# Stick-breaking attention inside a mixer block: another form for the score products, one pass for the value products, the scan in place

## The chip, the cores and the metric

The kernel runs on one core of one Trainium2 chip. A run's time is the device time of one execution in microseconds (us). The three runs of the kernel before are 2158.82, 2163.37 and 2165.51 us; their median, 2163.37 us, is the time that the change is measured against.

## The reference

A model block of width 1024 works on 512 positions. Its input projection feeds two groups of eight heads of 64 columns each: a recurrent group (RWKV-7 time mixing) and a stick-breaking attention group. Both outputs go through one output projection; a second model follows, of a conv layer and a neighbourhood-attention layer, each with an FFN. The change touches the stick-breaking group:

```python
q, k, v, g = jnp.split(p, 4, axis=-1)                  # 8 heads of 64 columns
z = jnp.einsum('bhqd,bhkd->bhqk', q_blk, k) / 8        # one block of 128 queries
mask = k_pos[None, :] < q_pos[:, None]                 # strictly causal
log_1m = jnp.where(mask, jax.nn.log_sigmoid(-z), 0.0)
after = lax.cumsum(log_1m, axis=3, reverse=True) - log_1m
attn = jnp.where(mask, jnp.exp(jax.nn.log_sigmoid(z) + after), 0.0)
o = jnp.einsum('bhqk,bhkd->bhqd', attn, v)             # then RMS norm per head, times silu(g)
```

The modulation vectors that several layers use (`mod = silu(c) @ w_ada + b_ada`) are the other place that the change touches.

## The kernel before, in words

Everything is float32. Large products are made of three f32r products of high and low parts (`mm3`, L171 to L173): a weight is loaded by DMA to `st`, ScalarE (ACT) casts it to a high part `wh` (L155), VectorE (DVE) subtracts to get the low part `wl` (L156), and TensorE (PE) adds hi*hi, lo*hi and hi*lo in one PSUM bank. Small products are plain f32; the profile shows each of those as two instructions on PE.

`block1` makes four recurrent pairs of heads (`rwkv_pair`, 0 to 3) and four attention pairs (`sb_pair`, 4 to 7) in the order of the table `ORDER`; then, from L435, the output projection. A scheduling layer sorts each engine's instructions ahead of time: what is written earlier has priority, and where that waits, the next ready work is put between. So the products of a later recurrent pair, or of the output projection, stand on PE between the steps of an attention pair. Each engine then runs its list in order.

An attention pair `p` goes like this. Two projections give q and k as plain f32 tiles (L1046). Every second pair makes the values `sbv`. A third projection gives the gate, on which ACT takes a sigmoid (L1069, L1070). Then come four query blocks i with two heads e each, eight rounds of one chain over the first n = 128(i+1) keys:

- PE: the score product (L1078), f32, in which the head's 64 rows of q and k are contracted, so on 64 of the array's 128 rows; then a bf16 product that adds the causal mask (L1079)
- ACT: two sigmoids out of PSUM (L1082, L1083)
- DVE: a memset of one column (L1085), a reversed running product into the tile `cum` (L1087), a product (L1089)
- PE: i+1 transposes (L1093); DVE for e = 0 or ACT for e = 1 copies them out of PSUM to `pt` (L1095)

The scores and the transposes share one PSUM bank (`ss`). After each query block its value products follow (L1100): 128 queries wide, f32, on 64 of the array's columns, one for each j up to i and each head. The pair ends in a norm (L1103 to L1111).

The modulation sums (`ada_load`, `ada_sum`, L193 to L209) are DVE work that is spread over `block1` at low priority and over the conv layer and the first FFN (`step`, two jobs at a time): GpSimd (POOL) issues a DMA of one 128x1024 row block to the tile `ast` (two buffers), and DVE reduces it in two halves, for each of one or two condition vectors.

Of the kernel before, what the change touches and what calls it, by code (L numbers as in the profile page):

```python
# [15 lines left out]
D = 1024  # L16
KT = 8
S = 512
# [66 lines left out]
class K:  # L85
# [98 lines left out]
    def cact(self, i):  # L184
# [3 lines left out]
        t = self.ap.tile([128, D], F32, tag="ast", name="ct", bufs=2)  # L188
        nc.scalar.activation(t, c, AF.Tanh, scale=0.5)
        nc.vector.scalar_tensor_tensor(c, t, 1.0, c, op0=ALU.add, op1=ALU.mult)  # L190
        return c

    def ada_load(self, src, cbs, mod, bname, j):  # L193
        st = self.ap.tile([128, D], F32, tag="ast", name="ast", bufs=2)
        self.nc.gpsimd.dma_start(st, src)  # L195
        return st, cbs, mod, bname, j

    def ada_sum(self, job, after=None):
        st, cbs, mod, bname, j = job
        for hf in range(2):  # L200
            hs = slice(512 * hf, 512 * hf + 512)
            for r, c in enumerate(cbs):
# [3 lines left out]
                    out=junk, in0=st[:, hs], in1=c[:, hs], scale=0.5, scalar=o if hf else self.V(bname, j),  # L206
# [105 lines left out]
    def block1(self):  # L312
# [524 lines left out]
    def rwkv_pair(self, p, W, h, zl, omu, oka, pre):  # L837
# [45 lines left out]
        XY = T("XY", (128, NCH, 2, CH), 2)  # L883
# [152 lines left out]
    def sb_pair(self, p, W, h, sbt):  # L1036
# [4 lines left out]
        qk = []  # L1041
        for i in range(2):
            t = sb.tile([128, S], F32, tag=f"qk{i}", name=f"qk{i}")
            ps = self.psum("acc")
            self.gemm(ps, W[17 + 4 * i + p], h)
            nc.scalar.mul(t, ps, 0.125 if i == 0 else 1.0)  # L1046
            qk.append(t)
        q, k = qk
# [17 lines left out]
        pg = self.psum("acc")  # L1066
        self.gemm(pg, W[25 + p], h)
        gs = sb.tile([128, S], F32, tag="sgs", name="sgs")
        nc.scalar.activation(gs, pg, AF.Sigmoid)  # L1069
        TT(gs, gs, pg, ALU.mult)  # L1070
        po = self.psum("so")
        for i in range(4):
            n = 128 * (i + 1)
            pts = []
            for e in range(2):
                r = slice(64 * e, 64 * e + 64)
                pz = self.psum("ss")
                mm(pz[:, :n], lhsT=q[r, 128 * i:n], rhs=k[r, :n], start=True, stop=False)  # L1078
# [11 lines left out]
                pT = self.psum("ss")  # L1090
# [115 lines left out]
```

## Time and profile before

The profile is of one execution: its span, from first to last instruction, is 2157.0 us. No device time of this execution stands beside it; the median of the runs is 6.4 us above the span.

| what | value |
|---|---|
| runs, median | 2163.37 us |
| profiled execution, span | 2157.0 us |
| PE busy | 2099.8 us, 97% of the span |
| DVE busy | 1237.6 us, 57% |
| ACT busy | 805.3 us, 37% |
| granted TensorE clock, mean | 0.990 |
| first score product, last score product | at 122 us and 489 us |

PE is the engine that nearly always works; a PE matmul's duration includes its way through the array, so the distance from one start to the next tells what it costs in a row of matmuls. DVE is busy for a little over half of the whole, but for much more in the attention stretch.

### The profile page before, as it was taken

What the parts mean: (1) busy time and instruction counts of PE and PEld (TensorE: products, weight loads), DVE (VectorE), ACT (ScalarE), POOL (GpSimd) and SP (SyncE); (2) the same over time, 40 slices, a digit from 0 to 9 for tenths busy, and PEclk for the clock granted to TensorE, in tenths of its full rate; (3) what the DMA queues carried; (4) which work ended last, traced back from release to release, by engine and by line L of the source; (5) the groups of instructions that cost most, each with busy time, mean ns of one, the idle gap of its engine ahead of it and who ended that gap; (6) DMA issues with size and microseconds to landing.
All of it is one profiled execution on the core that took longest, in us unless ns stands there. A gap on an engine that the chain in (4) does not pass through costs nothing.

```text
span 2157.0 us, 34034 instructions
## 1 busy us (share of the span) xinstructions
PE 2099.8 (97%) x13824; PEld 1673.6 (78%) x13824; DVE 1237.6 (57%) x2598; ACT 805.3 (37%) x1503; POOL 173.8 (8%) x241
## 2 busy tenths in 40 slices
PE   6999999998999999999999999899999999999999
PEld 3676667665788887888888888797777777888887
DVE  2869886657987738643453454525554545434443
ACT  3436444346322225221221222416565635323232
POOL 0000000003200001000000000101222211000000
PEclk9999999999999999999999999999999999999999
DMA  7432322113344412331332232121110112232323
GB/s 269 145 100 89 109 71 79 34 46 99 109 153 149 147 50 98 123 122 65 122 115 88 101 120 83 63 69 59 40 58 32 45 59 79 98 98 95 100 97 99
DMA packets 61934, 203.62 MB, mean 94 GB/s; under 512 B 6993, under 2 KB 9041, under 8 KB 61777
## 3 DMA queue, kind: packets, MB, share of 16 engines
q1 hardware_dynamic: 46800, 146.92, 20.1%
q0 software_dynamic: 14976, 54.53, 7.4%
q8 instruction: 108, 1.77, 0.3%
q14 instruction: 50, 0.40, 0.1%
HBM read 199.32 MB, written 2.10 MB: 93 GB/s over the span
## 4 chain that ended last, share of the span: by engine, by line
PE 89%; DVE 5%; ACT 3%; DMA 1%; issue 1%; SPq 0%; POOL 0%; ACTq 0%; DVEq 0%; POOLq 0%
PE acc L172 19%; PE acc L173 19%; PE acc L171 19%; PE cacc L173 5%; PE cacc L172 5%; PE cacc L171 5%; PE py L826 2%; DVE nt L285 2%; PE sm L804 2%; PE pT L817 2%; PE sm L802 1%; PE ss L1078 1%; PE so L1100 1%; PE G L910 1%; PE py L1014 1%
## 5 line engine op out<-in xcount | busy, mean ns | idle before, releaser
L155 ACT CAST wh<-st 128x512 fp32r<-128x512 f32 (+2 forms) x481 | 292.2, 609 | 721.8 <-PE acc L172 283.2
L156 DVE TENSOR_TENSOR wl<-st,wh 128x512 fp32r<-128x512 f32 (+2 forms) x481 | 324.0, 676 | 352.5 <-ACT wh L155 350.1
L171 PE MATMUL acc<-xzzh,wh 128*128 128x512 f32 x352 | 138.7, 394 | 0.0
L173 PE MATMUL acc<-xzzh,wl 128*128 128x512 f32 x352 | 138.0, 392 | 0.0
L172 PE MATMUL acc<-xzzl,wh 128*128 128x512 f32 x352 | 138.0, 392 | 0.0
L205 DVE CUSTOM_DVE_ANT_0 junk<-ast,cb,vec 128x512 bf16<-128x512 f32 x168 | 125.2, 745 | 3.3 <-DMA ast<-in_w_ada_dram 1.9
L205 DVE CUSTOM_DVE_ANT_0 junk<-ast,cb,m 128x512 bf16<-128x512 f32 x168 | 125.4, 747 | 2.3
L195 POOL DMA_DIRECT2D ast<-in_w_ada_dram x96 | 50.8, 529 | 865.4 <-DVE m L205 781.0
L173 PEld LDWEIGHTS acc<-xzzh,wl 128*128 128x128 f32 x352 | 66.0, 188 | 14.8
L171 PEld LDWEIGHTS acc<-xzzh,wh 128*128 128x128 f32 x352 | 66.1, 188 | 13.5 <-issue 0.5
L172 PEld LDWEIGHTS acc<-xzzl,wh 128*128 128x128 f32 x352 | 66.1, 188 | 13.5 <-issue 0.5
L171 PE MATMUL acc<-h0h,wh 128*128 128x512 f32 (+1 forms) x164 | 66.1, 406 | 4.2 <-ACT h0h L292 2.9
L172 PE MATMUL cacc<-czzl,wh 128*128 128x256 f32 x240 | 68.0, 284 | 0.0
L172 PE MATMUL acc<-h2l,wh 128*128 128x512 f32 (+1 forms) x164 | 66.2, 404 | 1.7 <-DVE h2l L293 1.7
L171 PE MATMUL cacc<-czzh,wh 128*128 128x256 f32 x240 | 67.5, 281 | 0.0
L172 PE MATMUL acc<-h1l,wh 128*128 128x512 f32 (+1 forms) x164 | 66.9, 408 | 0.6 <-POOL h1l L290 0.5
L173 PE MATMUL cacc<-czzh,wl 128*128 128x256 f32 x240 | 67.4, 281 | 0.0
L172 PE MATMUL acc<-h0l,wh 128*128 128x512 f32 (+1 forms) x164 | 66.2, 404 | 0.3 <-DVE h0l L293 0.3
L171 PE MATMUL acc<-h4h,wh 128*128 128x512 f32 (+1 forms) x164 | 65.3, 398 | 1.2 <-ACT h4h L292 0.8
L173 PE MATMUL acc<-h2h,wl 128*128 128x512 f32 (+1 forms) x164 | 66.2, 404 | 0.0
L172 PE MATMUL acc<-h6l,wh 128*128 128x512 f32 (+1 forms) x164 | 65.4, 399 | 0.7 <-DVE h6l L293 0.7
L173 PE MATMUL acc<-h0h,wl 128*128 128x512 f32 (+1 forms) x164 | 66.1, 403 | 0.0
(783 smaller groups left out, 5672.8 us busy)
## 6 DMA issues: line engine op xcount, KB each, us to landing
ast<-in_w_ada_dram POOLq DMA_DIRECT2D x96, 512.0 KB, 4.0
st<-in_ffn_w_in_dram SPq DMA_DIRECT2D x88, 512.0 KB, 3.5
st<-in_ffn_w_out_dram SPq DMA_DIRECT2D x32, 448.0 KB, 3.3
st<-in_w_in_dram SPq DMA_DIRECT2D x24, 512.0 KB, 3.5
st<-in_conv_w_in_dram SPq DMA_DIRECT2D x24, 512.0 KB, 4.4
ast<-in_ada_n_dram SPq DMA_DIRECT2D x16, 512.0 KB, 9.0
st<-in_ffn_w_out_dram SPq DMA_DIRECT2D x16, 512.0 KB, 3.5
st<-in_w_qk_dram SPq DMA_DIRECT2D x16, 512.0 KB, 3.5
```

The lines of the kernel that those rows point to most:

```text
L155: nc.scalar.copy(hi[:, :n], sl)
L156: nc.vector.tensor_tensor(lo[:, :n], sl, hi[:, :n].bitcast(F32), ALU.subtract)
L171: mm(out, lhsT=lh, rhs=rh, start=first, stop=False)
L172: mm(out, lhsT=lh, rhs=rl, start=False, stop=False)
L173: mm(out, lhsT=ll, rhs=rh, start=False, stop=last)
L195: self.nc.gpsimd.dma_start(st, src)
L205: i = self.nc.vector.tensor_tensor_reduce(out=junk, in0=st[:, hs], in1=c[:, hs], scale=0.5, scalar=o if hf else self.V(bname, j), op0=ALU. ...
L285: nc.vector.scalar_tensor_tensor(t, xs[k], gain[:, k:k + 1], rstd, op0=ALU.mult, op1=ALU.mult)
L802: mm(o[e], lhsT=qh[:, e, qs], rhs=ks(kk[:, e]), start=True, stop=False)
L804: mm(o[e], lhsT=ql[hv[e], qs], rhs=ks(kk[hv[e], e]), start=False, stop=True)
L817: nc.tensor.transpose(pT[:, i], s[:, 128 * i:128 * i + 128], self.C("ident"))
L826: mm(g(po[64 * e:64 * e + 64]), lhsT=vb, rhs=pr.rearrange("p (a t) -> p a t", a=2) if j == 0 else pr, start=n == 0, stop=n == 3)
```

## The change

Scores. q and k are kept as high and low f32r parts. The keys of a pair lie in tiles of two slots, one for each head; the other head's 64 rows of a slot are zero (written once by POOL). Each score product becomes three f32r products that contract all 128 rows. The two parts of q take one ACT and one DVE instruction, those of k two and two on 64 rows each.

Scan. The running product is written over its input, `om`, and the product that follows takes it shifted by one column; the tile `cum` and its memset are gone.

Values. The transposed weights of all four query blocks are kept, ordered by key block, and the value products come after the eighth round: one for each key block and head, 512, 384, 256 and 128 queries wide. The copies out of PSUM are made in two pieces where i > 1.

Gate. Its projection and sigmoid stand behind the value products.

Space. `XY` of the recurrent pairs has one buffer in place of two. A modulation row comes as two half rows in two 512-column tiles; `ast` has still two buffers, which now hold one row together. The tanh of the condition vectors goes by halves.

```diff
     def ada_load(self, src, cbs, mod, bname, j):
-        st = self.ap.tile([128, D], F32, tag="ast", name="ast", bufs=2)
-        self.nc.gpsimd.dma_start(st, src)
+        st = []
+        for hs in (slice(0, 512), slice(512, D)):
+            t = self.ap.tile([128, 512], F32, tag="ast", name="ast", bufs=2)
+            self.nc.gpsimd.dma_start(t, src[:, hs])
+            st.append(t)
...
+            self.kz = [[sb.tile([128, 2, S], F32R, name=f"kz{n}") for n in "hl"]]
+            for t in self.kz[0]:
+                nc.gpsimd.memset(t[64:128, 0].bitcast(F32), 0.0)
+                nc.gpsimd.memset(t[0:64, 1].bitcast(F32), 0.0)
...
-        XY = T("XY", (128, NCH, 2, CH), 2)
+        XY = T("XY", (128, NCH, 2, CH))
...
-            nc.scalar.mul(t, ps, 0.125 if i == 0 else 1.0)
+        nc.scalar.mul(qh, ps, 0.125)
+        STT(ql, ps, 0.125, qh.bitcast(F32), op0=ALU.mult, op1=ALU.subtract)
...
+        for e, r in enumerate(hv):
+            nc.scalar.copy(kh[r, e], ps[r])
+            TT(kl[r, e], ps[r], kh[r, e].bitcast(F32), ALU.subtract)
...
-                mm(pz[:, :n], lhsT=q[r, 128 * i:n], rhs=k[r, :n], start=True, stop=False)
+                mm(pz[:, :n], lhsT=qh[:, qs], rhs=kh[:, e, :n], start=True, stop=False)
+                mm(pz[:, :n], lhsT=qh[:, qs], rhs=kl[:, e, :n], start=False, stop=False)
+                mm(pz[:, :n], lhsT=ql[:, qs], rhs=kh[:, e, :n], start=False, stop=False)
...
-                cum = sbt.tile([128, S + 1], F32, tag="zc", name="cum", bufs=2)
-                nc.vector.memset(cum[:, n:n + 1], 1.0)
-                rv = cum[:, :n][:, ::-1]
-                nc.vector.tensor_tensor_scan(rv, om[:, :n][:, ::-1], self.one.to_broadcast([128, n]), 1.0,
+                rv = om[:, :n][:, ::-1]
+                nc.vector.tensor_tensor_scan(rv, rv, self.one.to_broadcast([128, n]), 1.0,
...
-                TT(sg[:, :n], sg[:, :n], cum[:, 1:n + 1], ALU.mult)
+                TT(sg[:, :n - 1], sg[:, :n - 1], om[:, 1:n], ALU.mult)
...
-            for j in range(i + 1):
-                for e in range(2):
-                    cc = (p % 2) * 128 + 64 * e
-                    mm(po[64 * e:64 * e + 64, 128 * i:n], lhsT=v[:, j, cc:cc + 64],
-                       rhs=pts[e][:, 128 * j:128 * j + 128], start=j == 0, stop=j == i)
+                cp = nc.scalar.copy if e else nc.vector.tensor_copy
+                m = min(i + 1, 2)
+                cp(pts[e][:, i:i + 3 * m - 2:3], pT[:, :m])
+                if i > 1:
+                    cp(pts[e][:, 5 + i:8 + 2 * (i - 2)], pT[:, 2:i + 1])
+        for j in range(4):
+            for e, r in enumerate(hv):
+                cc = (p % 2) * 128 + 64 * e
+                mm(po[r, 128 * j:], lhsT=v[:, j, cc:cc + 64],
+                   rhs=pts[e][:, at[j]:at[j] + 4 - j].rearrange("p a t -> p (a t)"), start=j == 0, stop=j == 3)
```

What it moves shows in each engine's list. On PE, in the first attention pair (4), before, from a transposed round of the second query block to the next score product (`qk` are q and k, `so` the attention output, `acc` a projection that fills in):

```order
L1093 MATMUL ss<-con,sg 128x128 x2
L173 MATMUL acc<-h4h,wl 128x512
...
L1078 MATMUL ss<-qk_1450,qk_1413 128x256
L1079 LDWEIGHTS bcon
L1079 MATMUL ss<-bcon 128x128
L1100 MATMUL so<-pt,sbv 64x128
L172 MATMUL acc<-h6l,wh 128x512
```

The same pair now, its last round and the value products after it (line numbers of the changed kernel: L1085 to L1087 the scores, L1088 the mask, L1099 the transposes, L1109 the value products):

```order
L1085 MATMUL ss<-kzh,sqh 128x512
L1086 MATMUL ss<-kzl,sqh 128x512
L1087 MATMUL ss<-kzh,sql 128x512
L1032 MATMUL rsm<-BK_1464,con 128x512
L1088 LDWEIGHTS bcon
L1088 MATMUL ss<-bcon 128x128
L171 MATMUL acc<-h0h,wh 128x512
...
L1099 MATMUL ss<-con,sg 128x128 x4
...
L1109 MATMUL so<-pt_1684,sbv 64x512
L1109 MATMUL so<-pt_1683,sbv 64x384
L1109 MATMUL so<-pt_1684,sbv 64x384
```

A score product's neighbours are now products on the full array; the value products, which stood in eight groups for each pair, stand in two.

On ACT, in the last attention pair (7), before, where a norm of the recurrent pair 3 falls between two rounds (L232 and L240 are its logarithm and exponential, `Z` their tile):

```order
L234 ACT_TABLE_LOAD
L232 ACTIVATE Z<-rsm,epsb 128x512
L240 ACTIVATE Z<-Z 128x512
L1082 ACT_TABLE_LOAD
L1082 ACTIVATE sg<-ss 128x512
L1083 ACTIVATE om<-ss 128x512
```

And now (L236 and L244 are the norm, L1091 and L1092 the sigmoids):

```order
L1091 ACTIVATE sg<-ss 128x512
L1030 ACTIVATE BK_4877<-BK_4881 128x512
L238 ACT_TABLE_LOAD
L236 ACTIVATE Z<-rsm,epsb 128x512
L1092 ACT_TABLE_LOAD
L1092 ACTIVATE om<-ss 128x512
L244 ACT_TABLE_LOAD
L244 ACTIVATE Z<-Z 128x512
...
L1091 ACT_TABLE_LOAD
```

The norm's two functions now stand on both sides of the second sigmoid, with a table load ahead of each step. Over the whole of ACT's list the loads go up by nine.

On DVE, in the conv layer, the sums of one modulation row now (L209 a sum, `vec` in its operands marks the first half, `m_0` the second; the names behind "waits" are the semaphores, DMASW those of POOL's DMAs, DMAHW those of SP's):

```order
L209 ISA junk,m_0_70<-ast,cb_487,vec 128x512 [waits DMASW0_49,DVE_49]
L209 ISA m_0_70 128x1
L156 TENSOR_TENSOR wl<-st,wh 128x512 [waits PE_49,Activation_49]
L209 ISA junk,m_0_70<-ast,cb_495,vec 128x512 [waits DVE_49]
L209 ISA m_0_70 128x1
L209 ISA junk,m_0_70<-ast,cb_487,m_0_70 128x512 [waits DMASW1_49,DVE_49]
L209 ISA m_0_70 128x1
L209 ISA junk,m_0_70<-ast,cb_495,m_0_70 128x512 [waits DVE_49]
```

Their places are nearly those of before, but the sum that opens the second half (the sixth row) waits for a DMA of its own, which before was not there: the whole row came with one.

More of the change, by code (lines that the diff above doesn't have):

```diff
@@ L205, in ada_sum @@
                 i = self.nc.vector.tensor_tensor_reduce(
-                    out=junk, in0=st[:, hs], in1=c[:, hs], scale=0.5, scalar=o if hf else self.V(bname, j),
+                    out=junk, in0=st[hf], in1=c[:, hs], scale=0.5, scalar=o if hf else self.V(bname, j),
                     op0=ALU.mult, op1=ALU.add, accum_out=o)
@@ L1040, in sb_pair @@
         A = self.A
[L1041 to L1045, printed above, removed]
-            nc.scalar.mul(t, ps, 0.125 if i == 0 else 1.0)
-            qk.append(t)
-        q, k = qk
+        hv = [slice(0, 64), slice(64, 128)]
+        qh, ql = self.hl(sb, S, "sq")
+        ps = self.psum("acc")
+        self.gemm(ps, W[17 + p], h)
+        nc.scalar.mul(qh, ps, 0.125)
+        STT(ql, ps, 0.125, qh.bitcast(F32), op0=ALU.mult, op1=ALU.subtract)
+        kh, kl = self.kz[p % len(self.kz)]
+        ps = self.psum("acc")
+        self.gemm(ps, W[21 + p], h)
+        for e, r in enumerate(hv):
+            nc.scalar.copy(kh[r, e], ps[r])
+            TT(kl[r, e], ps[r], kh[r, e].bitcast(F32), ALU.subtract)
         if p % 2 == 0:
@@ L1065, in sb_pair @@
         v = self.sbv
[L1066 to L1071, printed above, removed]
+        pts = [sbt.tile([128, 10, 128], F32, tag=f"pt{e}", name=f"pt{e}") for e in range(2)]
+        at = (0, 4, 7, 9)
         for i in range(4):
             n = 128 * (i + 1)
-            pts = []
+            qs = slice(128 * i, n)
             for e in range(2):
-                r = slice(64 * e, 64 * e + 64)
                 pz = self.psum("ss")
-                mm(pz[:, :n], lhsT=q[r, 128 * i:n], rhs=k[r, :n], start=True, stop=False)
+                mm(pz[:, :n], lhsT=qh[:, qs], rhs=kh[:, e, :n], start=True, stop=False)
+                mm(pz[:, :n], lhsT=qh[:, qs], rhs=kl[:, e, :n], start=False, stop=False)
+                mm(pz[:, :n], lhsT=ql[:, qs], rhs=kh[:, e, :n], start=False, stop=False)
                 mm(pz[:, n - 128:n], lhsT=self.bcon[:, 0:128], rhs=self.bcon[:, 128:256], start=False, stop=True)
@@ L1088, in sb_pair @@
                                              op0=ALU.mult, op1=ALU.mult)
[L1089 to L1090 removed]
+                TT(sg[:, :n - 1], sg[:, :n - 1], om[:, 1:n], ALU.mult)
+                pT = self.psum("ss", (128, 4, 128))
                 for j in range(i + 1):
[L1092 to L1094 removed]
@@ L1095, in sb_pair @@
-                (nc.scalar.copy if e else nc.vector.tensor_copy)(pt[:, :n], pT[:, :n])
-                pts.append(pt)
-            for j in range(i + 1):
-                for e in range(2):
-                    cc = (p % 2) * 128 + 64 * e
-                    mm(po[64 * e:64 * e + 64, 128 * i:n], lhsT=v[:, j, cc:cc + 64],
-                       rhs=pts[e][:, 128 * j:128 * j + 128], start=j == 0, stop=j == i)
+                    nc.tensor.transpose(pT[:, j], sg[:, 128 * j:128 * j + 128], self.C("ident"))
@@ L1102, in sb_pair @@
+        pg = self.psum("acc")
+        self.gemm(pg, W[25 + p], h)
+        gs = sbt.tile([128, S], F32, tag="zo", name="sgs", bufs=2)
+        nc.scalar.activation(gs, pg, AF.Sigmoid)
+        TT(gs, gs, pg, ALU.mult)
         sq = sbt.tile([128, S], F32, tag="zs", name="osq", bufs=2)
```

11 lines of the change are left out of this document (5 added, 6 removed).

## The prediction

> **What bounds the kernel now.** I read the page first, for the engine that works most; then the table by stretches, since the change touches only the attention pairs (122 to about 500 us) and the modulation sums (up to about 1310 us).
>
> ```profile
> PE 2099.8 (97%) x13824; PEld 1673.6 (78%) x13824; DVE 1237.6 (57%) x2598; ACT 805.3 (37%) x1503; POOL 173.8 (8%) x241
> ```
>
> ```profile
> 120.00:180.00 60.00, 60.00 (x363) 38.69 (x362) 46.59 (x128) 26.16 (x57) 3.17 (x6) 1.00 0.28 92
> 180.00:340.00 160.00, 156.70 (x1992) 104.16 (x1991) 138.04 (x324) 80.05 (x152) 7.38 (x14) 0.99 0.27 90
> 340.00:500.00 160.00, 158.20 (x1517) 106.86 (x1516) 92.82 (x213) 67.26 (x143) 0.53 (x1) 1.00 0.17 54
> 560.00:760.00 200.00, 200.00 (x1146) 175.53 (x1146) 163.00 (x414) 52.14 (x97) 18.20 (x34) 1.00 0.44 150
> ```
>
> The columns of the table are the stretch, its length, the busy time of PE, of its weight loads, of DVE, ACT and POOL, then the granted clock and the DMA. TensorE works for 97% of the span. From 120 to 500 us it is busy for 374.9 of 380 us at a clock of 0.99 to 1.00, so what is taken off PE there comes off the end, as long as the others keep up. DVE is the one that may not: it is busy for 138.0 of 160 us (86%) in the middle of the attention and for 163.0 of 200 us (82%) in the conv layer, the last row.
>
> **What the change does, part by part.** A matmul's duration contains its way through the array, so I count from a start to the next start. The timeline of PE has the smallest and the largest score product (L1078, two instructions each) and what follows them:
>
> ```profile
> 141.36 0.48 PE L1078 MATMUL ss<-qk,qk 64*128 64x128 f32 x2
> 141.78 0.23 PE L1079 MATMUL ss<-bcon 128*128 128x128 bf16 x1
> 141.94 0.43 PE L1100 MATMUL so<-pt,sbv 128*64 128x128 f32 x2
> 142.30 0.50 PE L173 MATMUL acc<-h5h,wl 128*128 128x512 f32 x1
> ...
> 178.75 0.39 PE L171 MATMUL acc<-h6h,wh 128*128 128x512 f32 x1
> 178.98 0.40 PE L172 MATMUL acc<-h6l,wh 128*128 128x512 f32 x1
> 179.31 0.87 PE L1100 MATMUL so<-pt,sbv 128*64 128x128 f32 x10
> 180.10 1.12 PE L1078 MATMUL ss<-qk,qk 64*128 64x512 f32 x2
> 181.16 0.23 PE L1079 MATMUL ss<-bcon 128*128 128x128 bf16 x1
> 181.20 0.47 PE L173 MATMUL acc<-h6h,wl 128*128 128x512 f32 x1
> ```
>
> *Scores.* A score product takes 0.42 us with 128 keys (141.36 to 141.78) and 1.06 with 512 (180.10 to 181.16): a step of 0.213 for each further 128, so 0.107 for each of its two instructions. With the two sizes between, 0.42 + 0.63 + 0.85 + 1.06 = 2.96 us for one head, 23.7 for eight. An f32r product 512 wide takes 0.23 us before another (178.75 to 178.98); one 256 wide takes 0.11 to 0.12, as two of the conv layer's show:
>
> ```profile
> 560.04 0.28 PE L171 MATMUL cacc<-hc0h,wh 128*128 128x256 f32 x1
> 560.15 0.28 PE L172 MATMUL cacc<-hc0l,wh 128*128 128x256 f32 x1
> ```
>
> 384 wide I put halfway, at 0.175. No row has 128 wide: it costs between half of 0.12 and 0.12, and I take 0.11, near the top, since each product also loads 128 columns of weights. Three products of each size make 1.9 us for a head and 15.2 for eight. Saved: 8.5 us, and 9.7 with 0.06.
>
> *Changes of tiling.* The rows print the part of the array that a product uses, as rows*columns. Of two equal gemm products one takes 0.23 us when a 128*128 product follows, and the other 0.33 (178.98 to 179.31) when a 128*64 one does. The mask product takes 0.04 before a gemm (181.16 to 181.20) and 0.16 before a value product (141.78 to 141.94). A change therefore costs 0.10 to 0.12 us. The new scores use the full array like the gemms, the transposes and the mask. In the order 27 of the 32 old scores directly followed a gemm or a value product, where the change now falls away (2.7 us), and the mask stands before a change 10 times in place of 21 (1.3 us). Together 4.0 us, and 2 at the low end, if other neighbours change it instead. The Trainium skill, "TensorEngine Tiling (Array Packing)", section "Key Properties", says that a change of the tiling mode drains TensorE; by that rule the sum stays as it is, with the drain as its cause, and the two rows agree.
>
> *Value products.* They are f32 too, two instructions each, 128 queries wide. In each query block one stands alone, since its head is ready first: 0.36 us (141.94 to 142.30). The others follow in a group of 2, 6, 10 or 14 instructions. The ten take 0.79 us (179.31 to 180.10), less a change 0.69: at 0.107 each they would take 1.07, so the two heads, which use different column halves, run partly side by side. Four more instructions are two products of each head's kind, 0.213 us if the heads overlap fully; so I put the four groups at 0.36, 0.58, 0.79 and 1.0. With the four lone ones a pair takes 1.44 + 2.73 = 4.2 us, four pairs 16.7. After, head 0's product of 512 queries stands alone: 2 x 4 x 0.107 and a change, 0.96. Then head 1 has 512 + 384 + 256 + 128 = 1280 queries, 20 steps of 0.107 = 2.1, with the rest of head 0 beside it and two changes: 2.3. That is 3.3 for a pair and 13.2 for four: 3.5 less. If wide products don't overlap, head 0's other 768 queries cost 1.3 more, 4.6 a pair, which is 1.7 more in all than before. The new order alternates the heads as the old groups do, so I take the saving.
>
> PE in sum: 8.5 + 4.0 + 3.5 = 16.0 us less; at the low end 8.5 + 2.0 - 1.7 = 8.8.
>
> *DVE and ACT.* The split of q and k adds 12 subtractions on DVE, 8 of them on 64 rows, of the kind that makes `wl`; ACT gets nine more table loads by the order:
>
> ```profile
> L156 DVE TENSOR_TENSOR wl<-st,wh 128x512 fp32r<-128x512 f32 (+2 forms) x481 | 324.0, 676 | 352.5 <-ACT wh L155 350.1
> ```
>
> ```profile
> 133.26 1.28 ACT L1069 ACT_TABLE_LOAD   x1
> 134.55 0.60 ACT L1069 ACTIVATE sgs<-acc 128x512 f32<-128x512 f32 x1
> ```
>
> ```profile
> ACT sg L1082 <- PE ss L1079: 49.3, 24, 4.0
> ```
>
> DVE: 12 x 0.676 = 8.1 us over four pairs, and 8 more pieces of copies; the memsets that go are left out of the sum. In the middle stretch only one pair's split falls (2 us), on top of 138.0 of 160, so DVE stays short of full there: I take 2 us as lost, between 0 and 8.1. ACT: 9 x 1.28 = 11.5 us, and 1.28 is all that a load holds up here, since the sigmoid starts 0.01 us after it. ACT is half idle in the table above, and in 24 of the 32 rounds it waits for the score product, 49.3 us in all; a load that stands ahead of such a wait costs nothing. It costs where it stands between the two sigmoids, as in pair 7. I take two loads' worth, 2.6 us, between 0 and 11.5. The Trainium skill, "ScalarE: Activation LUTs", section "What ACT_TABLE_LOAD costs", adds a drain and gives 2.66 us for each change of set; by that the nine would hold ACT for 23.9 us and the two that I count would cost 5.3, an estimate from that page, with which the time below would be 2.7 us more. The two ACT rows show no such time behind the load; the measurement decides.
>
> *Half rows of modulation.* With two half-row buffers, the DMA of a half can start only when the half two before it has been summed; before, a whole row was between. In the conv layer the sums of the first halves of four rows begin and end like this (DVE's timeline; a READ_ACCUMULATOR ends a sum), and the fourth row's last sum, at 628.21, lets POOL issue the next DMA:
>
> ```profile
> 605.53 0.08 DVE L205 DVE_READ_ACCUMULATOR2_ANT m<- 128x1 f32 x1
> 609.06 0.75 DVE L205 CUSTOM_DVE_ANT_0 junk<-ast,cb,vec 128x512 bf16<-128x512 f32 x1
> ...
> 612.52 0.08 DVE L205 DVE_READ_ACCUMULATOR2_ANT m<- 128x1 f32 x1
> ...
> 614.71 0.75 DVE L205 CUSTOM_DVE_ANT_0 junk<-ast,cb,vec 128x512 bf16<-128x512 f32 x1
> ...
> 626.54 0.08 DVE L205 DVE_READ_ACCUMULATOR2_ANT m<- 128x1 f32 x1
> ...
> 628.13 0.08 DVE L205 DVE_READ_ACCUMULATOR2_ANT m<- 128x1 f32 x1
> 628.25 0.75 DVE L205 CUSTOM_DVE_ANT_0 junk<-ast,cb,vec 128x512 bf16<-128x512 f32 x1
> ```
>
> ```profile
> 628.51 0.53 POOL L195 DMA_DIRECT2D ast<-in_w_ada_dram  x1 [8.66 <-DVE m L205]
> ```
>
> ```profile
> ast<-in_w_ada_dram POOLq DMA_DIRECT2D x32, 512.0 KB, 3.8
> ...
> st<-in_w_qk_dram SPq DMA_DIRECT2D x16, 512.0 KB, 3.5
> ...
> bias<-in_rpb_dram SPq DMA_DIRECT2D x16, 256.0 KB, 2.6
> ```
>
> The gaps that a half's DMA would have are 3.45, 2.1 and 1.6 us (605.61 to 609.06, 612.60 to 614.71, 626.62 to 628.25), 7.2 in all. Where one is too short, DVE stands at that sum, the next `wl` is queued behind it, and PE's third product of a weight waits for `wl`. A whole row lands 3.8 us after its issue in this layer; on SP's queue 256 KB take 0.9 less than 512, so I put a half at 2.9, and 0.3 more until POOL issues (628.21 to 628.51). Against 3.2 us the gaps are short by 0, 1.1 and 1.6: DVE stands for 2.7 us in a conv tile of about 25 us, in which it is idle for 18%, 4.6 us. That idle time is the cover, so I cost this at nothing; without it, it would be 8 tiles x 2.7 = 22 us. `XY` with one buffer is costed at nothing too: each pair's `XY` is written behind the transposes that read the last one's, and behind those stands a full round of gemms.
>
> *Sum.* 16.0 - 2 - 2.6 = 11.4 us off the span of 2157.0: 2145.6. The median of the runs lies 6.4 us above that span, so 2152 us.
>
> **The rivals.**
>
> *Nothing is given back* (chance 0.12): fillers cover every load and subtraction, and 2163.4 - 16.0 = 2147.4 us. For it: from 120 to 500 us PE is idle for only 380 - 374.9 = 5.1 us now, so the fillers do cover the chains. Against it: with less PE work the same chains have less cover.
>
> *The rounds' chains bound it* (0.20): sigmoids, scan, product, transposes and copy are one chain through one PSUM bank, and PE's work was already put between. Then the loads count nearly whole: 16.0 - 2 - 11.5 = 2.5 us less, 2161 us. Against it stands ACT's wait of 49.3 us.
>
> *The products don't do what they should* (0.07): the value products don't overlap and the tilings change elsewhere, 8.8 - 2 - 2.6 = 4.2 us less, 2159 us.
>
> *DVE falls behind in the conv layer* (0.13, the slower side): if a half row lands later than about 3.7 us after its issue, the three gaps are short by 3 x 4.0 - 7.2 = 4.8 us a tile, more than DVE's idle 4.6, and from there each further microsecond costs PE 3 us in each of 8 tiles. At 4.5 us it is (3 x 4.8 - 7.2 - 4.6) x 8 = 21 us, so 2163.4 - 11.4 + 21 = 2173 us. For it: a half is not far below the whole row's 3.8. Against: 256 KB landed in 2.6 us on SP's queue.
>
> **How the numbers follow.** The forecast has 0.48; 2152 us is its time. It and the first rival are faster by over 0.3%, that is by over 6.5 us, about what a measurement of this kernel can tell from no change, as its three runs lie 0.3% apart: 0.60. The second and third rival lie within it: 0.27. The last is slower: 0.13. The range leaves out most of that rival and reaches from 2144 (nothing given back, and the runs' scatter of about 3 us) to 2166 (chains and the same scatter).
>
> **What would show it.** In the new profile the four scores of a head should take about 1.9 us from start to start, the gemm or transpose before them 0.23 rather than 0.33, and the value products 3.3 us a pair, in starts 0.01 us apart. PE from 120 to 500 us should lose 15 us of work and DVE's waits for `ast` should appear at 560 to 760 us without a PE wait there. The forecast is wrong if the last norm of the attention pairs ends less than 8 us earlier, or if PE waits for `wl` in the conv layer.

## The result: slower by 0.5%, and the profile after

The changed kernel takes 2176.64 us (median of 17 runs), the kernel before 2166.53 us (17 runs beside them): a ratio of 1.0053, with a 95% interval of 1.0033 to 1.0074. The forecast was 2152 us and faster, so it was wrong.

In the profiled execution after, the span is 2173.6 us and the device time 2175.36 us, so 1.8 us lie outside the span. The table by stretches, read as before (the last row is the conv layer's stretch, which now starts 13.7 us later):

```profile
120.00:180.00 60.00, 58.64 (x332) 37.09 (x331) 40.03 (x107) 29.54 (x63) 5.37 (x10) 0.87 0.26 87
180.00:340.00 160.00, 148.12 (x1926) 103.77 (x1925) 135.42 (x314) 78.45 (x144) 13.98 (x26) 0.98 0.26 85
340.00:500.00 160.00, 152.58 (x1497) 104.70 (x1495) 103.40 (x229) 76.23 (x160) 3.22 (x6) 0.99 0.17 54
574.00:774.00 200.00, 200.00 (x1146) 175.49 (x1145) 162.36 (x414) 53.10 (x97) 35.72 (x66) 1.00 0.46 150
```

TensorE is now idle for 1.4 + 11.9 + 7.4 = 20.7 us from 120 to 500 us, where it was 5.1, and its granted clock is 0.87 in the first of these stretches, where it was 1.00. The conv layer is untouched: 200.00 of 200 us busy at full clock.

To compare kernels, one stretch is cut out of each trace by its work: from the first small product of the first recurrent pair (`pQ`) to the first product of the conv layer (`cacc`). The row of this stretch before, and after:

```profile
95.70:531.80 436.10, 423.70 (x4619) 286.75 (x4619) 320.15 (x740) 204.56 (x406) 25.46 (x34) 0.99 0.25 82
```

```profile
93.50:545.10 451.60, 422.59 (x4551) 294.32 (x4551) 326.53 (x733) 218.42 (x428) 39.22 (x59) 0.96 0.25 79
```

The clock's records in the trace are either 1 or 0.5. Half of the time in which TensorE is busy at 0.5 is taken as what the half clock costs; the rest of its busy time is counted as work. So the stretch of these two executions comes apart like this:

| us | before | after | difference |
|---|---|---|---|
| TensorE's work at full clock | 418.5 | 405.9 | -12.6 |
| TensorE idle | 12.4 | 29.0 | +16.6 |
| cost of the half clock | 5.1 | 16.7 | +11.6 |
| length | 436.1 | 451.6 | +15.5 |

The saved work arrived. Idle time took it back, and then the clock took as much again. What lies ahead of the stretch is 2.2 us shorter, what lies behind it 3.1 us longer, 1.9 of these again by half clock; together that is the 16.6 us between the spans.

*The half clock.* The same 30 us after, in the table by stretches:

```profile
110.00:120.00 10.00, 10.00 (x144) 9.25 (x143) 6.06 (x14) 2.17 (x5) 1.61 (x3) 0.58 0.33 104
120.00:130.00 10.00, 10.00 (x49) 6.99 (x48) 4.26 (x10) 5.16 (x9) 0.00 (x0) 0.50 0.32 105
130.00:140.00 10.00, 10.00 (x65) 6.86 (x63) 5.75 (x15) 6.30 (x21) 1.08 (x2) 0.90 0.06 24
```

From 111.5 to 132.0 us, 20.5 us long, TensorE has half its clock, although its records show it busy all the time: a busy share of 10.00 of 10 hides 10 us of loss. Of the columns here, only the clock's shows it. Every such stretch in the traces is a multiple of 3.41 us, but for the last of each trace, which the program's end cuts off. The Trainium skill, "TensorE: Matmul & The Clock Gate", section "What's actually happening", says that a monitor decides by windows of 3.4 us and lets the clock up after one busy window; the length of the window agrees, the release does not: six windows in which the records show TensorE always busy passed here before the clock came back.

The scatter goes with the clock too. Over the 17 runs of the changed kernel the time goes from 2169 us at a mean clock of 0.987 to 2191 at 0.977 (correlation -0.97), and time multiplied by clock is 2139 us in the mean, with a standard deviation of 1.7.

Time multiplied by mean clock is the time less half of what was spent at half clock, so it compares two kernels without the half clock. For the kernel before it is 2138 to 2139 us, in the mean of each of the five sets of its runs that stand beside the experiments. So over all runs the saved work and the new idle time cancel to within about 1 us, and the 10 us between the two medians are nearly all half clock: the mean clock is 0.982 after and 0.987 to 0.989 before. Every ratio and mean leaves out two executions of run 1 that were in a slower state.

*A gap.* One of the two largest new gaps of TensorE, by its timeline, and what ACT did ahead of it:

```profile
303.37 0.79 PE L173 MATMUL acc<-h0h,wl 128*128 128x512 f32 x1 [3.44 <-DVE wl L156]
```

```profile
293.59 1.28 ACT L862 ACT_TABLE_LOAD   x1
294.88 0.60 ACT L862 ACTIVATE gs<-acc 128x512 f32<-128x512 f32 x1
295.50 1.28 ACT L878 ACT_TABLE_LOAD   x1
296.80 0.64 ACT L878 ACTIVATE PP<-t 128x512 f32<-128x512 f32 x1
297.45 1.28 ACT L886 ACT_TABLE_LOAD   x1
298.74 0.63 ACT L886 ACTIVATE kk<-kk 128x512 f32<-128x512 f32 x1
299.39 1.28 ACT L879 ACT_TABLE_LOAD   x1
300.69 0.63 ACT L879 ACTIVATE t<-t 128x512 f32<-128x512 f32 x1
```

Four loads stand among four functions with nothing idle between them, 5.1 us. The weight that TensorE needs next was cast before them, at 292.95 us; but in DVE's list its low part `wl` stands behind a step that waits for `kk`, and ACT ends `kk` only at 301.9 us. So TensorE waits 3.44 us for `wl`, and from 302.7 to 309.5 us it has half its clock: another 3.4 us.

### The profile page after: what moved, and what is told of

It reads as the page before. It is cut to its first block, busy times and chain, and to the rows that moved or that the text cites. A ratio compares the mean times of both kernels' runs of the same rounds, so it can differ in the third digit from the quotient of the medians.

```text
span 2173.6 us, 34258 instructions
## 1 busy us (share of the span) xinstructions
PE 2099.2 (97%) x13760; PEld 1682.1 (77%) x13760; DVE 1244.9 (57%) x2589; ACT 820.2 (38%) x1527; POOL 233.1 (11%) x349
## 4 chain that ended last, share of the span: by engine, by line
PE 73%; DVE 4%; ACT 3%; issue 1%; DMA 0%; POOL 0%; SPq 0%; ACTq 0%; DVEq 0%
PE acc L172 17%; PE acc L173 17%; PE acc L171 17%; PE cacc L173 5%; PE cacc L172 5%; PE cacc L171 5%; PE py L834 2%; PE sm L812 2%; PE pT L825 2%; DVE nt L289 2%; PE sm L810 1%; ACT wh L155 0%; PE pt L304 0%; PE so L1109 0%; DVE wl L156 0%
## 5 line engine op out<-in xcount | busy, mean ns | idle before, releaser
L198 POOL DMA_DIRECT2D ast<-in_w_ada_dram x192 | 103.4, 538 | 840.7 <-DVE m L209 766.5
L209 DVE CUSTOM_DVE_ANT_0 junk<-ast,cb,vec 128x512 bf16<-128x512 f32 x168 | 125.6, 747 | 42.1 <-DMA ast<-in_w_ada_dram 40.4
L209 DVE CUSTOM_DVE_ANT_0 junk<-ast,cb,m 128x512 bf16<-128x512 f32 x168 | 125.3, 746 | 23.4 <-DMA ast<-in_w_ada_dram 22.1
L173 PEld LDWEIGHTS acc<-xzzh,wl 128*128 128x128 f32 x352 | 66.0, 188 | 14.9
L171 PEld LDWEIGHTS acc<-xzzh,wh 128*128 128x128 f32 x352 | 66.1, 188 | 13.5 <-issue 0.5
L822 POOL TENSOR_SCALAR s<-s,st 128x512 f32<-128x512 f32 x64 | 44.3, 695 | 257.4 <-DVE st L821 248.4
L172 PE MATMUL acc<-h4l,wh 128*128 128x512 f32 (+1 forms) x164 | 66.1, 403 | 0.9 <-DVE h4l L297 0.8
```

What stands on the lines that cost most here:

```text
L171: mm(out, lhsT=lh, rhs=rh, start=first, stop=False)
L172: mm(out, lhsT=lh, rhs=rl, start=False, stop=False)
L173: mm(out, lhsT=ll, rhs=rh, start=False, stop=last)
L198: self.nc.gpsimd.dma_start(t, src[:, hs])
L209: i = self.nc.vector.tensor_tensor_reduce(out=junk, in0=st[hf], in1=c[:, hs], scale=0.5, scalar=o if hf else self.V(bname, j), op0=ALU.mul ...
L822: nc.gpsimd.tensor_scalar(s, s, st[:, 2:3], 1.0, op0=ALU.mult, op1=ALU.mult)
```

## The experiments

Each run was timed in five rounds beside the kernel before. Work, idle and half clock are of the stretch defined above, worked out from each run's trace in the same way; the loads are the table loads in ACT's whole list. The last column is time multiplied by mean clock, in the mean of all executions.

| run | what it is | ratio (95% interval) | loads | work | idle | half clock | time x clock |
|---|---|---|---|---|---|---|---|
| before | | 1 | 35 | 418.5 | 12.4 | 5.1 | 2138 to 2139 |
| after | the whole change | 1.0053 (1.0033 to 1.0074) | 44 | 405.9 | 29.0 | 16.7 | 2139 |
| 1 | after, loads grouped | 1.0029 (1.0007 to 1.0051) | 35 | 403.8 | 23.1 | 20.0 | 2133 |
| 2 | before + gate | 1.0105 (1.0086 to 1.0124) | 44 | 417.6 | 26.7 | 18.9 | 2151 |
| 3 | after, old scores | 1.0058 (1.0037 to 1.0079) | 38 | 412.1 | 19.5 | 12.1 | 2136 |
| 4 | after, old values | 1.0041 (1.0019 to 1.0064) | 43 | 413.4 | 24.5 | 9.0 | 2142 |
| 5 | before, no sums | 1.0024 (1.0004 to 1.0044) | 35 | 421.5 | 13.4 | 14.9 | 2141 |
| 6 | after, no sums | 0.9983 (0.9965 to 1.0002) | 42 | 409.5 | 19.1 | 15.7 | 2136 |
| 7 | before + space + scores | 0.9949 (0.9922 to 0.9977) | 37 | 412.2 | 13.9 | 11.7 | 2131 |
| 8 | before + half rows | 0.9958 (0.9935 to 0.9980) | 39 | 418.9 | 14.2 | 4.7 | 2139 |
| 9 | after, gate ahead of the scores | 1.0053 (1.0031 to 1.0076) | 44 | 409.9 | 24.1 | 13.1 | 2138 |
| 10 | before + gate, own tile | 1.0000 (0.9979 to 1.0022) | 35 | 416.7 | 13.8 | 10.5 | 2137 |
| 11 | after, gate in the output tile | 1.0022 (0.9999 to 1.0045) | 35 | 404.8 | 20.5 | 31.7 | 2134 |
| 12 | run 2, loads grouped | 1.0093 (1.0063 to 1.0123) | 36 | 413.8 | 25.8 | 26.0 | 2145 |
| 13 | before + space + values | 0.9958 (0.9940 to 0.9976) | 37 | 413.2 | 13.7 | 4.7 | 2132 |
| 14 | run 7, `XY` in two buffers | 0.9953 (0.9936 to 0.9970) | 37 | 412.4 | 14.7 | 11.6 | 2133 |
| 15 | run 7, whole rows | 1.0002 (0.9980 to 1.0024) | 41 | 414.3 | 15.8 | 12.1 | 2135 |
| 16 | after, gate first of all | 0.9931 (0.9902 to 0.9960) | 35 | 406.6 | 15.5 | 21.5 | 2131 |
| 17 | after, gate between blocks 2 and 3 | 1.0011 (0.9981 to 1.0041) | 35 | 407.5 | 20.9 | 13.2 | 2134 |

("Space" is the scan in place, `XY` in one buffer and half rows.) Work, idle and half clock are of one profiled execution each. From one execution to the next of a kernel time multiplied by clock has a standard deviation of 1.3 to 3 us; the half clock takes up the rest of the scatter, so its column can be off by several us. Runs 5 and 6 leave out sums, as told below, so they compute something else than the model.

### First theory: the table loads

Theory 1 said that sigmoids which fall between a preload and its use make chains of loads like the one above. Run 1 mends the order at the four places:

```diff
-        nc.scalar.activation(gs, pg, AF.Sigmoid)
+        gsa = nc.scalar.activation(gs, pg, AF.Sigmoid)
...
+        self.order(pre, gsa)
...
-        self.rsqrt(rs, pv, last, eps=1)
+        self.rse = self.rsqrt(rs, pv, last, eps=1)
...
-                nc.scalar.activation(sg[:, :n], pz[:, :n], AF.Sigmoid)
+                sa = nc.scalar.activation(sg[:, :n], pz[:, :n], AF.Sigmoid)
+                if (p, i, e) in ((0, 3, 1), (2, 0, 0), (3, 3, 0)):
+                    self.order(sa, self.rse)
```

> The changed kernel with ScalarE's order mended: the gate's sigmoid of a recurrent pair stands ahead of that pair's table preload, and three sigmoids of the attention rounds stand behind the exponential of the norm that they fell into. Its list has 35 table loads, as many as the kernel before, in place of 44; all else is as changed. Theory 1 (sigmoids between a preload and its use make chains of loads, TensorE idles behind them and then gets half its clock): idle time from about 95 us to the start of the conv layer falls from 34.8 to under 22 us, the two gaps of 2.9 and 3.4 us at 188 and 303 us go, and the time is 2150 to 2160 us, 0.2 to 0.7% below the kernel before. Theory 2 (the new form's own chains leave TensorE idle: split keys, value products held to the end, one buffer for XY): idle stays at 30 us or more, and the time stays 5 us or more above the kernel before.

Measured: 1.0029, idle 23.1 us. The nine loads are gone and so are the two gaps, but most of the idle time is still there, at other places. The theory holds for 6 of 16.6 us; time multiplied by clock falls by as much, from 2139 to 2133. Run 2 makes the gate's move alone, in the kernel before:

```diff
-        pg = self.psum("acc")
-        self.gemm(pg, W[25 + p], h)
-        gs = sb.tile([128, S], F32, tag="sgs", name="sgs")
-        nc.scalar.activation(gs, pg, AF.Sigmoid)
-        TT(gs, gs, pg, ALU.mult)
         po = self.psum("so")
...
+        pg = self.psum("acc")
+        self.gemm(pg, W[25 + p], h)
+        gs = sbt.tile([128, S], F32, tag="zo", name="sgs", bufs=2)
+        nc.scalar.activation(gs, pg, AF.Sigmoid)
+        TT(gs, gs, pg, ALU.mult)
         sq = sbt.tile([128, S], F32, tag="zs", name="osq", bufs=2)
```

> The kernel before with one edit of the change alone: the gate's projection and sigmoid stand behind the value products (its tile shares the buffers of the scan's input). Its list has 44 table loads in place of 35, like the changed kernel's. Scores, value products, scan, XY and modulation rows are as before. Theory 1: slower than the kernel before by 5 to 20 us, with new gaps of TensorE of 2 us or more behind loads. Theory 2: within 4 us of the kernel before.

Measured: 1.0105, 26.7 us idle, 44 loads. Such a small edit, in a kernel where no product has changed, costs twice what the whole change does. It fits theory 1, but run 12 takes eight of its loads away by the edit of run 1 (on the lines of the kernel before):

> The run of the gate alone (shared buffers, kernel before otherwise) with the order of ScalarE's sigmoids mended as in the first run, so 36 table loads in place of 44. Theory 1: close to the kernel before, within 5 us. Theory 4 (buffers or place, not the loads): 10 to 25 us slower than the kernel before.

Measured: 1.0093, 25.8 us idle. With eight loads fewer the time is nearly the same, though time multiplied by clock falls by 6 us here too, from 2151 to 2145. So the loads have a part, about 6 us in both pairs of runs, and are not the whole cause. The largest gap left in run 12, and what ACT did around its start:

```profile
181.48 1.09 PE L1091 MATMUL ss<-con,sg 128*128 128x128 f32 x4 [7.03 <-DVE sg L1087]
```

```profile
172.35 0.69 ACT L232 ACTIVATE Z<-rsm,epsb 128x512 f32<-128x512 f32 x1 [0.50 <-PE rsm L1025]
173.06 1.28 ACT L1078 ACT_TABLE_LOAD   x1
174.35 0.60 ACT L1078 ACTIVATE sg<-ss 128x512 f32<-128x512 f32 x1
174.97 1.28 ACT L240 ACT_TABLE_LOAD   x1
176.26 0.63 ACT L240 ACTIVATE Z<-Z 128x512 f32<-128x512 f32 x1
176.91 1.28 ACT L1081 ACT_TABLE_LOAD   x1
```

This gap stands behind loads as well: the two functions of a recurrent pair's norm (L232, L240) and the two sigmoids of the attention pair's seventh round (L1078, L1081) take turns, and the edit names the eighth round.

### The gate's tile

In its new place the gate takes one of the two buffers (`zo`) that the scan's inputs take in turn. Run 10 is run 2 with a tile for the gate alone:

```diff
-        gs = sbt.tile([128, S], F32, tag="zo", name="sgs", bufs=2)
+        gs = sb.tile([128, S], F32, tag="sgs", name="sgs")
```

> The kernel before with the gate behind the value products, as in the run of the gate alone, but the gate keeps a tile of its own and doesn't share the two buffers of the scan's input. 35 table loads in its list, against 44 with the shared buffers. Theory 4a (the shared buffers are what costs: the sigmoid has to wait for the last rounds and lands among loads): within 4 us of the kernel before. Theory 4b (the place itself, which takes 5.5 us of products from ahead of the rounds): 10 to 25 us slower, like the gate alone with shared buffers.

Measured: 1.0000, 13.8 us idle. The place costs nothing; the shared buffers cost the whole 1.05%. The groups of the gate's sigmoid show what they do. In run 2, then in run 10 (count, shortest/median/longest ns, first and last start):

```profile
L1100 ACT ACTIVATE sgs<-acc x4: 603/604/618, 189.1 to 512.1; 128x512 f32<-128x512 f32 x4
```

```profile
L1100 ACT ACTIVATE sgs<-acc x4: 591/594/607, 135.1 to 440.6; 128x512 f32<-128x512 f32 x4
```

With a tile of its own the first gate's sigmoid starts at 135.1 us, between the pair's first rounds: although it is written last, it is ready work and is put among them. With the shared buffers it has to wait until the rounds have given one back. It comes at 189.1 us, half a microsecond behind the start of the pair's last `om` sigmoid (188.6 us), when the pair's own norm and the next recurrent pair's preparation come too. The place in the text is the same in both runs; only the buffer makes the wait. What part of the cost comes by the nine loads that run 2 has and run 10 hasn't is not parted from the rest. In the changed kernel itself, where there is no room for another tile, run 11 keeps the gate in the pair's output tile:

```diff
+        y = self.yp.tile([128, S], F32, tag=f"y{4 + p}", name=f"y{4 + p}")
         pg = self.psum("acc")
         self.gemm(pg, W[25 + p], h)
-        gs = sbt.tile([128, S], F32, tag="zo", name="sgs", bufs=2)
-        nc.scalar.activation(gs, pg, AF.Sigmoid)
-        TT(gs, gs, pg, ALU.mult)
+        nc.scalar.activation(y, pg, AF.Sigmoid)
+        TT(y, y, pg, ALU.mult)
```

> The changed kernel with the gate at its new place, but kept in the pair's output tile in place of the shared buffers. 35 table loads against 44. Theory 4a: idle time falls below 20 us and the time is 5 to 15 us below the kernel before. Theory 4b: within 5 us of the changed kernel.

Measured: 1.0022. The idle time falls by 8.5 us, to 20.5, not below 20; the intervals of this run and of the changed kernel overlap. By time multiplied by clock it gains 5 us, with nine loads fewer. So in the whole change the shared buffers are one cause, and not the only one.

### The other parts by themselves

> The changed kernel with the scores put back to plain f32 on 64 rows (no split, no zero-padded keys); the rest is as changed. 38 table loads. By the prediction's sum the score products and tilings give back 8 to 12 us of TensorE work against the changed kernel, only the value products' 3.5 us are left of the gain. Theory 1: with six loads fewer the idle time falls below 25 us, so the time is 0 to 6 us below the kernel before, and so below the changed kernel's. Theory 2 with the split as the cause: the same. If idle stays at 30 us with few loads, another part is the cause and the time is 10 us or more above the kernel before.

> The changed kernel with the value products put back to one group for each query block, copies in one piece; scores, scan, gate, XY and half rows as changed. 43 table loads. Theory 1: as slow as the changed kernel or up to 4 us slower, 8 to 15 us above the kernel before, with gaps of 2 us or more behind loads. Theory 2 with the held value products as the cause: idle falls below 22 us and the time is below the kernel before.

Measured: 1.0058 and 1.0041, idle 19.5 and 24.5 us. Taking either part out of the changed kernel helps little, which fits the gate's tile staying in both. In run 3 the idle time falls as theory 1 had it, but the time does not. From the other side, each part was put into the kernel before. The edits are those of the change's diff:

> The kernel before with the new scores and what they need of space (scan in place, one buffer for XY, half rows); value products and gate stay as before. 37 table loads in its list, two more than before. Theory 1: with so few loads the gaps are few and the 8 to 12 us of TensorE work that the scores save arrive: 4 to 10 us below the kernel before. Theory 2: idle time after 95 us stays above 22 us and the time is at or above the kernel before.

> The kernel before with half rows of modulation in two half buffers, and nothing else of the change. Theory 3 in its narrow form (VectorE stands at sums whose half row has not landed, and this delays the rounds): 4 to 12 us slower than the kernel before, with new gaps of TensorE behind such waits. Theories 1 and 2: within 4 us.

> The kernel before with the value products of all query blocks at the pair's end, and the space for them (scan in place, one buffer for XY, half rows); scores in f32 and the gate ahead, as before. 37 table loads. Theory 5 (held to the end, the value products make a long tail of each pair: copy, products, square, norm, while the next recurrent pair waits on VectorE, and TensorE runs out of other work): idle time after 95 us above 19 us, and the time 4 to 20 us above the kernel before. Theory 1 (only orders with many table loads lose): idle below 16 us, and the time 5 to 10 us below the kernel before, as with half rows alone.

Measured: 0.9949, 0.9958 and 0.9958, idle about 14 us in all three. Half rows alone gain 0.4% with no work saved, which no theory had; by time multiplied by clock they are level with the kernel before (2139 and 2138 us), so their gain is less half clock (a mean clock of 0.992 against 0.987). Why they have less wasn't tested. The scores save 6.3 us of work and the values 5.3. The three ratios, whose intervals overlap, don't show these savings beside the half rows; time multiplied by clock does: 2131 and 2132 us, about 7 us less each, so both reach the end. Theory 5, that held value products make a tail, falls with run 13, and theory 3 in its narrow form with run 8. Two more runs part run 7:

> The kernel before with the new scores, the scan in place and half rows, but XY in two buffers; value products and gate as before. 37 table loads. If XY's buffer costs nothing: like run 7, 8 to 14 us below the kernel before. If one buffer costs in run 7: up to 6 us faster than run 7. Work of TensorE as in run 7, about 412 us after 95 us.

> The kernel before with the new scores, the scan in place and XY in one buffer, but whole rows of modulation; value products and gate as before. 41 table loads. If the gain of run 7 is the scores' saved work: 5 to 11 us below the kernel before. If it was the half rows' (another order, with fewer gaps): within 4 us of the kernel before, with idle above 18 us.

Measured: 0.9953 and 1.0002. One buffer or two for `XY` makes no difference. Without the half rows the scores' saved work is there (414.3 us), and 3 to 4 us of it by time multiplied by clock (2135), yet in time nothing is gained.

### VectorE's sums

Theory 3 blamed the modulation sums that fill VectorE's list. Both kernels were run without those of the attention (as the expectation says):

```diff
-            self.ada(A["ada_w"], [c0], self.m1, "ada_b", range(16, 24), 16)
+            nc.gpsimd.memset(self.m1[:, 16:24, :], 0.5)
...
-            self.ada(A["w_ada0"], c12, self.m2[0], "b_ada0", range(NA0))
+            nc.gpsimd.memset(self.m2[0][:, 0:NA0, :], 0.5)
```

> The kernel before without the modulation sums that lie in the attention: the 28 rows that are loaded by GpSimd and summed by VectorE there (96 sums, about 72 us of VectorE) are left out, their results set to 0.5; the conv layer's sums stay. It is the base for the next run. Theory 3 (VectorE's list, filled up with these sums, is what the gaps of the changed kernel come from): a little faster than the kernel before, by 2 to 8 us, since its TensorE idles for only 12 us there. Theory 2 (the chains themselves): the same.

> The changed kernel with the same sums left out. 42 table loads in its list, against 35 in the base. Theory 3: without the sums the gaps of 1 us and more go, the half clock with them, and the changed form is 8 to 16 us faster than the base without sums (the TensorE work that it saves). Theories 1 and 2 (chains of table loads, or the new form's own chains): gaps of 1 us or more stay and it is no more than 4 us faster than the base, or slower.

Measured: 1.0024 and 0.9983, so 0.4% apart, about 8 us: the lower end of what theory 3 named, and above the 4 us of the others. By time multiplied by clock the change is worth 5 us without the sums and nothing with them. The changed form's idle time falls by 10 us, to 19.1. Its gaps of 1 us and more are no longer more than its base has, 7.0 us in all against 7.2; the 5.7 us that it still idles more than its base (13.4) lie in shorter gaps. So the sums have a part in the large gaps, but the theory explains neither the rest of the idle time nor the half clock, which stayed (15.7 us). That the kernel before is even 0.2% slower without 60 us of VectorE's work, where theory 3 had it faster, shows how little an engine's load tells here.

### Where the gate stands

With scores and values together and the gate out of the shared buffers, only its place is left to choose. It was tried ahead of the scores (run 9), first of all the pair's work (run 16) and between the second and third query block (run 17), always in the output tile, as in run 11:

> The changed kernel with the gate's projection and sigmoid put back ahead of the scores; since no room is left for a tile of its own, the gate is kept in the pair's output tile. All else is as changed. 44 table loads in its list, as many as the changed kernel's. Theory 4 (the gate's new place costs what the scores and values gain): idle time after 95 us falls below 20 us and the time is 5 to 15 us below the kernel before. Theory 1 (the number of table loads decides): with 44 loads it is as slow as the changed kernel, 5 to 15 us above the kernel before.

> The changed kernel with the gate's projection and sigmoid written as the first work of a pair, ahead of the projections of q and k, and kept in the output tile; scores, values, scan, XY and half rows as changed. 35 table loads in its list. If the order of run 9 was only unlucky: idle after 95 us 16 us or less, TensorE's work about 406 us, and the time 10 to 18 us below the kernel before. If scores and values together leave too little cover: idle 20 us or more, and the time at most 5 us below the kernel before.

> The same as the run before, but the gate's projection and sigmoid are written between the second and the third query block. 35 table loads. The same two outcomes: idle of 16 us or less and 10 to 18 us below the kernel before if only the order decides, idle of 20 us or more and at most 5 us below if there is too little cover.

Measured: 1.0053, 0.9931 and 1.0011. Run 16 has every saving of the change and the lowest median of all, 2146.48 us against 2162.12 for the kernel before beside it, so 15.6 us less. It beats both kernels. Against the scores alone (run 7) no gain is shown: the intervals overlap, and time multiplied by clock is 2131 us in both. The stretch's rows of runs 9 and 16:

```profile
94.40:541.50 447.10, 423.01 (x4552) 291.25 (x4552) 327.91 (x734) 218.07 (x428) 39.70 (x60) 0.97 0.26 80
```

```profile
93.10:536.80 443.70, 428.15 (x4559) 295.91 (x4559) 328.60 (x734) 206.91 (x419) 39.13 (x60) 0.95 0.25 80
```

Engine by engine they do the same work; ACT's 11 us more in run 9 are nine loads. That run 9 is as slow as the changed kernel, with as many loads, is what theory 1 had said; theory 4 had it 5 to 15 us faster than the kernel before. Run 9 idles 447.10 - 423.01 = 24.1 us, run 16 443.70 - 428.15 = 15.5, and that although the profiled execution of run 16 was its slowest of nine (2160.90 us), by the half clock. Run 9's largest gap stands ahead of the third recurrent pair's products `G`, where `XY` is late:

```profile
299.62 0.79 PE L918 MATMUL G<-RA,XY 64*128 64x128 f32 x2 [6.21 <-DVE XY L899]
```

In run 16 the same products start at 296.92 us with no wait in front. The timelines of VectorE show a difference. In run 9 it works from 283.5 to 299.5 us with no wait of over 0.3 us, and five modulation sums (L209), 3.7 us in all, stand between the steps that lead to `XY`; four of them in a row:

```profile
285.17 0.75 DVE L209 CUSTOM_DVE_ANT_0 junk<-ast,cb,vec 128x512 bf16<-128x512 f32 x1
285.96 0.75 DVE L209 CUSTOM_DVE_ANT_0 junk<-ast,cb,vec 128x512 bf16<-128x512 f32 x1
286.76 0.75 DVE L209 CUSTOM_DVE_ANT_0 junk<-ast,cb,m 128x512 bf16<-128x512 f32 x1
287.56 0.75 DVE L209 CUSTOM_DVE_ANT_0 junk<-ast,cb,m 128x512 bf16<-128x512 f32 x1
288.23 0.54 DVE L890 TENSOR_SCALAR t<-t,vec,oka 128x512 f32<-128x512 f32 x1
```

In run 16 no sum stands there from 284 us until `XY` is made, and the norm of the attention pair comes behind it. Why one order of the same instructions is sorted this way and another isn't isn't settled: run 17 has as few loads as run 16 and a gap of 3.4 us at this place. Too little cover by itself is ruled out by run 16, which has as little work on TensorE as the changed kernel.

So no single part carries the 16.6 us. The loads (6 us of idle time, run 1), the gate's buffers (8.5, run 11) and the sums (10, run 6) overlap, and another order of the same work takes away 13.5 (run 16).

## Why the prediction was wrong

- *What bounds the kernel*: right, as far as it goes: TensorE is busy for 94% of the stretch after the change too. But the time is TensorE's work, its idle time and its clock, and the sum followed only the first two.
- *Scores*, 8.5 us less and most of 4.0 for the tiling: mis-sized, 6.3 in place of up to 12.5 (run 7). A round's rows in the changed kernel:

```profile
405.22 0.49 PE L918 MATMUL G<-RA,XY 64*128 64x128 f32 x2
405.63 0.39 PE L1085 MATMUL ss<-kzh,sqh 128*128 128x256 f32 x1
405.85 0.28 PE L1086 MATMUL ss<-kzl,sqh 128*128 128x256 f32 x1
405.97 0.28 PE L1087 MATMUL ss<-kzh,sql 128*128 128x256 f32 x1
406.09 0.23 PE L1088 MATMUL ss<-bcon 128*128 128x128 bf16 x1
406.25 0.93 PE L918 MATMUL G<-RA,XY 64*128 64x128 f32 x6
```

  The second and third product take the 0.12 us forecast for 256, and by the same reading about 0.11, 0.175 and 0.235 for the other sizes. The first takes 0.22: 17 of the 32 first products stand behind a product of another tiling, here `G`, and pay the 0.1 us, 1.7 in all. The prediction counted the neighbours of the old scores; the new list gave the new scores others. The rest of the 6 us that are missing isn't traced.
- *Value products*, 13.2 us for four pairs, 3.5 less: the overlap is right; alone they saved 5.3 us of work (run 13). A pair's second group takes 2.30 us, as forecast, in four of four pairs:

```profile
189.28 2.37 PE L1109 MATMUL so<-pt,sbv 128*64 128x512 f32 x14
191.58 0.50 PE L173 MATMUL acc<-h0h,wl 128*128 128x512 f32 x1
```

- *PE in sum*, 16.0 us less, 8.8 at the low end: 12.6 in the stretch.
- *Half rows*: right, and nearly to the figure. A half row landed in 3.0 us (forecast 2.9), and in the conv layer DVE stood for 23.6 us (forecast 8 x 2.7 = 22), as its waits there say, with TensorE at 200.00 of 200 us. The rival of a DVE that falls behind in the conv layer is refuted:

```profile
DVE junk L209 <- DMA ast<-in_w_ada_dram: 23.6, 27, 2.5
```

```profile
ast<-in_w_ada_dram POOLq DMA_DIRECT2D x192, 256.0 KB, 3.0
```

- *One buffer for `XY`*, costed at nothing: right beside the scores alone (runs 7 and 14).
- *DVE and ACT*, "I take 2 us as lost" and "two loads' worth, 2.6 us": this is the step that failed. Instead of 4.6 us, 16.6 us of idle time came, more than the work that was saved. The loads alone are worth about 6 us (run 1). And the sum priced each added instruction where it stood and never asked what the gate's new tile would wait for, although the diff shows that the tile shares the two buffers of the scan's input; runs 2 and 10 put that at 1.05% in the kernel before. ACT's wait of 49.3 us for the score product, which was named as the loads' cover, was no cover for what stands at the joints between pairs, where the two largest gaps are; the wait itself fell to 29.5 us:

```profile
ACT sg L1091 <- PE ss L1088: 29.5, 18, 4.2
```

- *The half clock* was no term of the sum at all. It cost 11.6 us between the two profiled executions, and over all runs it makes nearly the whole difference between the medians. The mean clock of 0.990 that stands ahead of the prediction is 21 us of the span of 2157, and the prediction gave it no price. The 6.4 us between the span and the median were taken for time around the span; 1.8 of them are, as the profile after shows. With 1.8 us the span of 2157.0 is the fastest of the three runs, 2158.82 us, so the rest is in all likelihood the clock.
- *The rivals*: the one on the slower side gave 2173 us, near the measured time, but by luck: DVE in the conv layer, its mechanism, costs nothing (above). The second, that the rounds' chains bound it, came closest in kind (less work, more idle, no gain), but gave 2161 us and took 11.5 us of loads for the price, of which runs 1 and 12 bear out about half.
- *What would show it*: the sign set for a wrong forecast came. The last norm of the attention pairs, which was to end at least 8 us earlier, ends 9.4 us later (510.5 us in place of 501.0, by the `y<-ors,sgs` of L1125 and L1111).

## What to carry to other kernels

A tile that moves into a ring of buffers brings a wait with it: ask what holds that ring at the new place, above all when a scheduler would have used the work as filler. In a kernel like this one, where TensorE is 97% busy, more idle time went with more half clock in the mean of the runs, and the busy time doesn't show the second; read work, idle and clock as three sums, and compare kernels by time multiplied by clock as well. A slower list may be cured by moving a few lines, so before a saving of TensorE work is given up, try the moved work at the other end of the block.

## What the runs showed of the hardware

TensorE's half clock lasted up to 27.3 us at a stretch (run 6, with TensorE busy for 26.9 of them); the 20.5 us of the changed kernel have no break in the records. It spread the runs of the changed kernel over 22 us, those of run 1 over 26. Of the 18 traces besides that of before, the ten with over 19 us of idle time in the stretch paid 17.6 us to the half clock in the mean, the other eight 11.5. Idle time isn't all that sets it: runs 7, 11, 14 and 16 and the changed kernel have a half clock of 20.5 us within 4 us behind gaps of 1.3 to 2.4 us near 110 us, and the kernel before, with a gap of 1.9 us there, one of only 3.4 us, and run 4, with a gap of 2.2 us, none. Whether the 32x32 products of that place keep the clock down wasn't tried.
